# Scores as four 64x64 products per chunk, and sums over channels as two-part products

## The chip, the cores and the metric

The kernel runs on one core of one Trainium2 chip. The metric is the device time of one execution in microseconds (us). Three timed runs of the kernel before gave 2873.15, 2877.79 and 2878.57 us; the median is 2877.79 us. One further execution was recorded by the hardware profiler, and every row below is from that one.

## The reference

One layer of a decoder over 2048 new tokens of one sequence, and over one new token of each of 8 other sequences. In outline:

```
h = rms_norm(x);  P = h @ w_in
branch A (16 heads of 64 channels; state S per head, 64x64, token by token):
  kk = k * k_k;  kk = kk * rsqrt(sum over the head's channels of kk*kk)
  S_t = S_{t-1} diag(w_t) + (S_{t-1} a_t) b_t^T + v_t k_t^T ;  y_t = S_t r_t,   a = -kk, b = kk * iclr
  y = group norm of y over the head's 64 channels
  bonus = (sum over the head's channels of r * k * r_k) * v
  A = ((y + bonus) * silu(z)) @ w_branch_r
branch B: GLU -> depthwise convolution, 31 taps, 512 channels -> layer norm over the 512 channels
  -> swish, * silu(z_c), @ w_branch_c
x + rms_norm((sigmoid(g_r) * A + sigmoid(g_c) * B) @ w_out)
```

So there are five sums over channels: two before the scan of a head and two after it (mean and variance), each over 64 channels, and the layer norm's mean and variance over 512.

## The kernel before

Channels lie on the 128 partitions and tokens along the free axis. The prompt is cut into 4 blocks of 512 tokens. In a block, two heads (128 channels) make a **unit**; there are 8 units in a block and 32 in all, counted here from 0 to 31. For a unit, 8 chunks of 64 tokens each are turned into matrix products.

A unit is one long chain over the engines. Its parts, with the names by which rows show them:

- the low-rank products (`pa<-tw,w`), then sigmoid, scan and exponentials on ScalarE (ACT) and VectorE (DVE);
- the sum of squares of kk (`pa<-tmp,ones_b`), and the sum for the bonus (`pa<-raw,ones_b`), each one product of a 128x128 block of ones with a 128x512 tile: `stat`. The stretch from the end of the unit ahead to this second sum is called the *front* below;
- the scores (`pa<-ar,bk`), masked on DVE into the tiles `sc`; for each chunk and each head one product with 64 rows and 128 columns of weights;
- the inverse of a triangular block: about 45 short instructions on DVE over `gd` and `zr`, at whose end PE continues with `pb<-gd,sc`;
- the *back*: `pb<-zbuf,gp`, `pa<-aw,zbuf`, `pa<-sc,pz`, then the states chunk by chunk (`pc<-xs,aw`), then the mean (`py<-gt,cent`) and the variance (`pc<-gt,ones_b`) of y.

Products on `fp32` tiles go through TensorE (PE) as two instructions. Tiles of type `fp32r` go through as one; exactness is had by splitting a tile into a rounded part and a remainder (`split`: a copy on ACT, a subtraction on DVE). The large projections (`gemm`, rows `pg<-ht,w`) are done so: three products for each pair of 128 rows and columns.

The program is written in the order: unit j, then the projections of unit j+1 (`unit_in`: 4 x 24 products), then what `FILL0`, `FILL1`, `FILL2` list for j: gates (digits, 48 products each), `u` (a GLU), `n` (`conv_norm`, the layer norm), `z` and `Z` (48 products each). A scheduler then orders each engine's instructions by what is ready, and earlier work first; the projections are thereby laid into the times in which the chain of the unit is on ACT and DVE. They are called the **fill** below. PE then runs its list in order.

Buffers are had from pools by tag, in the order of the program: a tag with one buffer (any that `BUFS`, L70, does not list) gives it to the next user when the one ahead has done. PSUM: `pg` has 3 banks (projections and `conv_norm`), `pa` 2, `pb`, `pc` and `py` 1 each.

`conv_norm` (L727) sums four convolution tiles (`cs`) over channels with four products on `avg_c` into one PSUM tile, subtracts the mean, squares each tile on ACT, and sums the squares with four products more. `FILL0` has it behind unit 4 of block 0, the other lists behind unit 2 of their blocks: units 4, 10, 18 and 26.

Of the kernel before, what the change touches and what calls it, by code (L numbers as in the profile page):

```python
# [8 lines left out]
F32 = mybir.dt.float32  # L9
# [16 lines left out]
def rwkv7_conformer_step(  # L26
# [6 lines left out]
    nc = tc.nc  # L33
# [55 lines left out]
    def new(shape, tag, dt=F32):  # L89
        return sb.tile(shape, dt, name=tag, tag=tag, bufs=BUFS.get(tag, 1))  # L90
# [14 lines left out]
    def stt(out, a, s, b, op0, op1):  # L105
        return nc.vector.scalar_tensor_tensor(out=out, in0=a, scalar=s, in1=b, op0=op0, op1=op1)  # L106
# [61 lines left out]
    def cmem(shape, v, name):  # L168
        t = const.tile(shape, F32, name=name)
        nc.gpsimd.memset(t, v)  # L170
        return t
# [5 lines left out]
    ones_b = cmem([128, 128], 0.0, "ones_b")  # L177
    avg_c = cmem([128, 128], 1.0 / DC, "avg_c")
# [36 lines left out]
    cent = const.tile([128, 128], F32, name="cent")  # L215
# [3 lines left out]
    stt(cent, ones_b, -1.0 / 64, ident, ALU.mult, ALU.add)  # L219
# [73 lines left out]
    gate_s = const.tile([128, 2 * KT, NS], F32, name="gate_s")  # L293
    mg_s = const.tile([128, 2, KT, NS], F32R, name="mg_s")
# [79 lines left out]
    def stat(pool, mat, src):  # L374
        ps = pool()
        mm(ps[:, 0:src.shape[1]], mat, src)
        return ps[:, 0:src.shape[1]]

# [92 lines left out]
    def unit(b, j, tw, ins):  # L471
# [4 lines left out]
        w2 = new([128, 3, 128], "w2", F32R)  # L476
        w2r = new([128, 3, 128], "wraw")
        nc.sync.dma_start(out=w2r, in_=w_lora[j])
        cp(w2, w2r)
        tt(w2[:, 2], w2r[:, 2], f32(w2[:, 2]), ALU.subtract)  # L480

        def lora(i):
            ps = pa()
            mm(ps, w2[:, i], tw[:, i], stop=False)
            mm(ps, w2[ES[i], 2], tw[ES[i], i], start=False)
            return ps
# [16 lines left out]
        rsqrt(kkn, stat(pa, ones_b, kkn), eps_kk)  # L503
# [4 lines left out]

        bk = new([128, NC, 3, C], "bk")
        mul(bk[:, :, 0, :], c3(kkn), c3(em))  # L510
        cp(bk[64:128, :, 2, :], bk[64:128, :, 0, :])
# [6 lines left out]
        mul(bonv, stat(pa, ones_b, R), V)  # L518
# [20 lines left out]
        for hf in range(2):  # L539
            pse = [pa(), pa()]  # L540
            for i in range(4):
                c = hf * 4 + i
                for e, es in enumerate(ES):
                    mm(pse[e][:, i * 128:i * 128 + 128], bk[es, c, e:e + 2].rearrange("p a t -> p (a t)"),
                       ar[es, c].rearrange("p a t -> p (a t)"))
            for e in range(2):
                mul(W[hf][:, :, e, :], pse[e].rearrange("p (c t) -> p c t", t=128),
                    maskw.unsqueeze(1).to_broadcast([128, 4, 128]))
# [77 lines left out]
        P = new([128, NC, C], "pz")  # L626
# [49 lines left out]
        pcen = stat(pyt, cent, ys)  # L676
        act(ys, pcen, AF.Square)
        rsqrt(ys, stat(pct, ones_b, ys), eps_gn, scale=1.0 / 64)
# [48 lines left out]
    def conv_norm(b, cs):  # L727
        ps = pgt()
        for ct in range(CT):
            mm(ps, avg_c, cs[ct], start=(ct == 0), stop=(ct == CT - 1))  # L730
        for ct in range(CT):
            tt(cs[ct], cs[ct], ps, ALU.subtract)
        ps = pgt()
        for ct in range(CT):
            sq = new([128, BS], "tmp")
            act(sq, cs[ct], AF.Square)
            mm(ps, avg_c, sq, start=(ct == 0), stop=(ct == CT - 1))
        rs = new([128, BS], "tmp")
        rsqrt(rs, ps, eps_ln)
        for ct in range(CT):  # L740
            mul(cs[ct], cs[ct], rs)
            s1 = new([128, BS], "tmp")
            sigmoid(s1, cs[ct], nscale=nlng[:, ct:ct + 1], nbias=nlnb[:, ct:ct + 1])
            act(cs[ct], cs[ct], AF.Identity, scale=pv("lng", ct), bias=pv("lnb", ct))
            mul(cs[ct], cs[ct], s1)
# [484 lines left out]
```

## Time and profile before

| | |
|---|---|
| median of three runs | 2877.79 us |
| profiled execution | 2879.12 us |
| its span, first to last instruction | 2877.4 us |
| PE busy | 2756.7 us (96%) |
| DVE busy | 1947.1 us (68%) |
| ACT busy | 1343.8 us (47%) |
| mean granted clock of PE | 0.985 |

PE is busy nearly all the time. A PE row `x32` of fp32 products stands for 16 of them, since each is two instructions. In a timeline the starts of rows of one engine tell how long a group took: the duration of a product includes the time until its result has landed, which the next one does not wait for.

### The profile page before, as it was taken

The numbers are of one execution on the slowest core, as the hardware profiler recorded it, in microseconds if no ns is written. First come the engines' busy times: TensorE is split into PE (matmuls) and PEld (weight loads), VectorE is DVE, ScalarE is ACT, GpSimd is POOL, SyncE is SP. The second block draws the span as 40 slices with busy tenths as digits, with TensorE's granted clock in tenths as the row PEclk, the third lists the DMA queues.
The fourth block names the chain that finished last, engine by engine and source line by source line (L and its number), as shares of the span: only waits on it lengthen the run. The fifth ranks groups of instructions, "written<-read, shape, count | busy, mean of one in ns | idle before, by whom it ended". The sixth has DMA issues, their size and how long they took to land.

```text
span 2877.4 us, 53953 instructions
## 1 busy us (share of the span) xinstructions
PE 2756.7 (96%) x21830; PEld 2198.1 (76%) x21830; DVE 1947.1 (68%) x4501; ACT 1343.8 (47%) x2822; POOL 15.6 (1%) x60
## 2 busy tenths in 40 slices
PE   6999899989999999997999999999999999999998
PEld 5888787877877777775787777777798776777777
DVE  5888787767777556676766767665866766566632
ACT  5555556654244455454213446455511446455521
POOL 0000000000000000000000000000000000000000
PEclk9999899999999999997999999999999999999999
DMA  6555554546874324343576334343566532333474
GB/s 236 175 180 186 187 171 133 180 156 210 304 279 131 117 97 159 128 138 107 172 255 208 124 127 138 124 137 100 182 199 218 187 121 77 99 103 118 130 264 160
DMA packets 158285, 468.90 MB, mean 163 GB/s; under 512 B 19857, under 2 KB 25218, under 8 KB 158027
## 3 DMA queue, kind: packets, MB, share of 16 engines
q1 hardware_dynamic: 155665, 456.50, 47.5%
q10 hardware_dynamic: 2370, 8.95, 0.8%
q8 instruction: 172, 2.82, 0.4%
q14 instruction: 78, 0.64, 0.1%
HBM read 352.50 MB, written 113.35 MB: 162 GB/s over the span
## 4 chain that ended last, share of the span: by engine, by line
PE 65%; DVE 20%; ACT 10%; DMA 2%; issue 2%; SPq 0%; POOL 0%; DVEq 0%; ACTq 0%; POOLq 0%
PE pg L112 40%; PE pa L112 12%; PE pc L112 4%; DVE gd L100 4%; DVE zr L576 4%; PE py L112 4%; DVE zr L106 3%; PE pb L112 2%; ACT sc L94 2%; ACT tmp L94 2%; DVE raw L106 1%; ACT zbuf L94 1%; ACT gp L94 1%; ACT gd L94 1%; DVE w L100 1%
## 5 line engine op out<-in xcount | busy, mean ns | idle before, releaser
L112 PE MATMUL pg<-ht,w 128*128 128x512 f32 (+1 forms) x7320 | 1521.4, 361 | 25.2 <-ACT ht L94 7.5
L112 PEld LDWEIGHTS pg<-ht,w 128*128 128x128 f32 x7320 | 1183.2, 189 | 262.3 <-issue 43.9
L106 DVE SCALAR_TENSOR_TENSOR et<-u,cw,et 128x512 f32<-128x512 f32 x480 | 359.3, 748 | 7.5
L94 ACT ACTIVATE raw<-pg,omm 128x512 f32<-128x512 f32 (+1 forms) x160 | 95.9, 600 | 292.9 <-PE pg L112 286.4
L100 DVE TENSOR_TENSOR gd<-zr,gp 128x8 f32<-128x8 f32 (+14 forms) x480 | 179.7, 374 | 12.8
L94 ACT ACTIVATE tmp<-tmp 128x512 f32<-128x512 f32 (+1 forms) x304 | 183.9, 624 | 9.0 <-DVE tmp L492 4.2
L112 PE MATMUL pg<-orr,w 128*128 128x512 f32 (+2 forms) x960 | 186.8, 350 | 0.0
L576 DVE TENSOR_REDUCE zr<-gd 128x2 f32<-128x8 f32 (+14 forms) x480 | 176.6, 368 | 12.3
L94 ACT ACTIVATE w<-wraw 128x512 fp32r<-128x512 f32 (+1 forms) x194 | 117.1, 609 | 129.8 <-PE pg L112 91.8
L112 PEld LDWEIGHTS pg<-orr,w 128*128 128x128 f32 x960 | 154.9, 188 | 25.9 <-issue 0.5
L662 DVE TENSOR_SCALAR xs<-pc,dk 128x64 f32<-128x64 f32 x224 | 63.6, 284 | 142.5 <-PE pc L112 141.8
L112 PEld LDWEIGHTS pa<-ar,bk 64*128 64x128 f32 x1024 | 120.0, 196 | 40.9 <-issue 19.1
L106 DVE SCALAR_TENSOR_TENSOR raw<-pg,prm,raw 128x511 f32<-128x511 f32 (+2 forms) x192 | 106.4, 567 | 52.0 <-ACT raw L94 51.0
L100 DVE TENSOR_TENSOR w<-wraw,w 128x512 fp32r<-128x512 f32 (+1 forms) x194 | 119.6, 621 | 31.3 <-ACT w L94 28.4
L112 PE MATMUL pa<-ar,bk 64*128 64x128 f32 x1024 | 136.1, 294 | 2.5 <-DVE sc L100 2.5
L100 DVE TENSOR_TENSOR aw<-pa,id 128x256 f32<-128x256 f32 x64 | 27.2, 424 | 148.8 <-PE pa L112 148.3
L106 DVE SCALAR_TENSOR_TENSOR zr<-zr,sub 128x5 f32<-128x5 f32 (+7 forms) x512 | 115.7, 226 | 13.4
L94 ACT ACTIVATE gd<-sc 32x128 f32<-32x128 f32 x256 | 78.4, 306 | 83.0 <-DVE sc L100 79.2
L94 ACT ACTIVATE x<-pg 128x512 f32<-128x512 f32 (+1 forms) x80 | 40.8, 511 | 158.8 <-PE pg L112 153.7
L100 DVE TENSOR_TENSOR sc<-pa,maskw 128x512 f32<-128x512 f32 x128 | 87.0, 688 | 34.3 <-PE pa L112 33.2
L94 ACT ACTIVATE sc<-pa 64x256 f32<-64x256 f32 (+1 forms) x192 | 72.9, 380 | 52.6 <-PE pb L112 49.6
L100 DVE TENSOR_TENSOR x<-x,pg 128x512 f32<-128x512 f32 (+1 forms) x80 | 46.1, 578 | 71.9 <-PE pg L112 59.5
(331 smaller groups left out, 3686.4 us busy)
## 6 DMA issues: line engine op xcount, KB each, us to landing
w<-kept_in SPq DMA_DIRECT2D x366, 512.0 KB, 3.3
kept_in<-w SPq DMA_DIRECT2D x122, 512.0 KB, 4.5
wraw<-in_w_in_dram SPq DMA_DIRECT2D x122, 256.0 KB, 3.1
w<-kept_br SPq DMA_DIRECT2D x48, 512.0 KB, 3.6
w<-kept_out SPq DMA_DIRECT2D x40, 512.0 KB, 4.4
gate<-x SPq DMA_DIRECT2D x64, 256.0 KB, 3.3
x<-gate SPq DMA_DIRECT2D x64, 256.0 KB, 4.2
orr<-in_x_prompt_dram SPq DMA_DIRECT2D x24, 512.0 KB, 6.7
```

Source lines behind the costliest of these rows:

```text
L94: return nc.scalar.activation(out=out, in_=in_, func=func, scale=scale, bias=bias, **kw)
L100: return nc.vector.tensor_tensor(out=out, in0=a, in1=b, op=op)
L106: return nc.vector.scalar_tensor_tensor(out=out, in0=a, scalar=s, in1=b, op0=op0, op1=op1)
L112: return nc.tensor.matmul(out=out, lhsT=lhsT, rhs=rhs, start=start, stop=stop, **kw)
L576: nc.vector.tensor_reduce(out=zr[:, 0:n, t:t + 2], in_=pr[:, 0:n, :, 0:w], axis=AX.X, op=ALU.add)
L662: nc.vector.tensor_scalar(out=state[:, j, :] if c == NC - 1 else xs[:, c + 1, :], in0=pu[:, c * C:c * C + C], scalar1=dk[:, c:c + 1], scal ...
```

## The change

Four parts:

1. `stat2` takes the place of `stat` for the four sums of a unit: the source is split into two `fp32r` parts in a tile `st` (one buffer), and two products take the place of one on fp32.
2. The scores: for each chunk and head two products of 64x64 weights instead of one of 64x128. The copy on ACT that put one operand in a second place goes.
3. `conv_norm` adds its four tiles (and then their four squares) on DVE, and makes one `stat2` of each sum.
4. The low-rank weights lie in a constant tile whose unused quarters are zero; `P` of a unit takes the tag `gt` in place of one of its own.

```diff
@@ lora weights and two-part constants @@
-    cent = const.tile([128, 128], F32, name="cent")
+    cent_r = const.tile([128, 128], F32R, name="cent")
...
+    lora_w = const.tile([128, 4, 128], F32R, name="lora_w")
+    nc.gpsimd.memset(f32(lora_w), 0.0)
...
+    def stat2(pool, mat, src):
+
+        parts = new([128, 2, BS], "st", F32R)
+        split(parts[:, 0], parts[:, 1], src)
+        ps = pool()
+        for i in range(2):
+            mm(ps, mat, parts[:, i], start=(i == 0), stop=(i == 1))
+        return ps
@@ unit @@
-        w2 = new([128, 3, 128], "w2", F32R)
+        w2 = lora_w
         w2r = new([128, 3, 128], "wraw")
         nc.sync.dma_start(out=w2r, in_=w_lora[j])
-        cp(w2, w2r)
-        tt(w2[:, 2], w2r[:, 2], f32(w2[:, 2]), ALU.subtract)
+        cp(w2[:, 0:2], w2r[:, 0:2])
+        for i, es in enumerate(ES):
+            tt(w2[es, 2 + i], w2r[es, 2], f32(w2[es, i]), ALU.subtract)
...
-            mm(ps, w2[ES[i], 2], tw[ES[i], i], start=False)
+            mm(ps, w2[:, 2 + i], tw[:, i], start=False)
...
-        rsqrt(kkn, stat(pa, ones_b, kkn), eps_kk)
+        rsqrt(kkn, stat2(pa, ones_r, kkn), eps_kk)
...
-        bk = new([128, NC, 3, C], "bk")
+        bk = new([128, NC, 2, C], "bk")
         mul(bk[:, :, 0, :], c3(kkn), c3(em))
-        cp(bk[64:128, :, 2, :], bk[64:128, :, 0, :])
...
-        mul(bonv, stat(pa, ones_b, R), V)
+        mul(bonv, stat2(pa, ones_r, R), V)
...
-                for e, es in enumerate(ES):
-                    mm(pse[e][:, i * 128:i * 128 + 128], bk[es, c, e:e + 2].rearrange("p a t -> p (a t)"),
-                       ar[es, c].rearrange("p a t -> p (a t)"))
+                for q in range(2):
+                    for e, es in enumerate(ES):
+                        mm(pse[e][ES[e ^ q], i * 128:i * 128 + 128], bk[es, c, q, :],
+                           ar[es, c].rearrange("p a t -> p (a t)"))
...
-        P = new([128, NC, C], "pz")
+        P = new([128, NC, C], "gt")
...
-        pcen = stat(pyt, cent, ys)
+        pcen = stat2(pyt, cent_r, ys)
         act(ys, pcen, AF.Square)
-        rsqrt(ys, stat(pct, ones_b, ys), eps_gn, scale=1.0 / 64)
+        rsqrt(ys, stat2(pct, ones_r, ys), eps_gn, scale=1.0 / 64)
@@ conv_norm @@
-        ps = pgt()
-        for ct in range(CT):
-            mm(ps, avg_c, cs[ct], start=(ct == 0), stop=(ct == CT - 1))
+        sm = new([128, BS], "tmp")
+        tt(sm, cs[0], cs[1], ALU.add)
+        for ct in range(2, CT):
+            tt(sm, sm, cs[ct], ALU.add)
+        ps = stat2(pgt, avg_r, sm)
         for ct in range(CT):
             tt(cs[ct], cs[ct], ps, ALU.subtract)
-        ps = pgt()
-        for ct in range(CT):
+        sm = new([128, BS], "tmp")
+        act(sm, cs[0], AF.Square)
+        for ct in range(1, CT):
             sq = new([128, BS], "tmp")
             act(sq, cs[ct], AF.Square)
-            mm(ps, avg_c, sq, start=(ct == 0), stop=(ct == CT - 1))
+            tt(sm, sm, sq, ALU.add)
+        ps = stat2(pgt, avg_r, sm)

```

How this moves PE's instructions in block 3, from the sum for the bonus of unit 26 to the end of its inverse. Before:

```order
L112 MATMUL pa<-raw,ones_b 128x512
L112 MATMUL pa<-ar,bk 128x128 x8
L112 MATMUL pg<-ht,w 128x512 x2
L112 MATMUL pa<-ar,bk 128x128 x8
L112 MATMUL pg<-ht,w 128x512 x6
L112 MATMUL pa<-ident,ar 64x64 x16
L112 MATMUL pa<-xv,sc 64x64 x16
L617 MATMUL pa<-ident,bk 128x128 x4
L112 MATMUL pg<-ht,w 128x512 x2
L617 MATMUL pa<-ident,bk 128x128 x4
L112 MATMUL pg<-ht,w 128x512 x85
L112 MATMUL pb<-gd,sc 32x32 x16
```

After, on PE, from the mean of unit 25 to the same place and two rows past it:

```order
L112 MATMUL py<-st,cent 128x512 x2
L112 MATMUL pc<-st,ones_b 128x512 x2
L112 MATMUL pa<-st,ones_b 128x512 x4
L112 MATMUL pa<-ar,bk 64x128 x32
L112 MATMUL pa<-ident,ar 64x64 x16
L112 MATMUL pa<-xv,sc 64x64 x16
L630 MATMUL pa<-ident,bk 128x128 x8
L112 MATMUL pb<-gd,sc 32x32 x16
L112 MATMUL pb<-zbuf_183,gp 32x32 x16
L112 MATMUL pa<-aw,zbuf_183 64x128 x16
```

The rows `pg<-ht,w`, the fill, stood at four places of this stretch, 95 products in all; there is none now.

The second place is `conv_norm` of block 3 on PE. Before, its first four products stood by the end of the inverse of unit 25:

```order
L112 MATMUL pg<-ht,w 128x512 x66
L112 MATMUL pg<-et,avg_c 128x512
L112 MATMUL pb<-gd,sc 32x32 x16
L112 MATMUL pg<-et,avg_c 128x512 x2
L112 MATMUL pb<-zbuf_184,gp 32x32 x16
L112 MATMUL pg<-et,avg_c 128x512
L112 MATMUL pa<-aw,zbuf_184 64x128 x16
```

After, it stands behind the variance of unit 26, a whole unit later, and the fill follows it:

```order
L112 MATMUL pc<-xs,aw 64x64 x2
L112 MATMUL py<-aw,xs 64x64 x2
L112 MATMUL py<-st,cent 128x512 x2
L112 MATMUL pc<-st,ones_b 128x512 x2
L112 MATMUL pg<-st,avg_c 128x512 x4
L112 MATMUL pg<-ht,w 128x512 x82
```

The DVE rows of the same place, after, with the tiles' numbers: `st` is the tile of `stat2`, and the three users of it here are the mean of unit 26, its variance, and the first sum of `conv_norm` (`tmp_25063`, whose additions stand a unit earlier on DVE).

```order
L675 TENSOR_SCALAR state_189<-pc_24768,dk_24465 128x64
L100 TENSOR_TENSOR st_24844<-gt_24842,st_24844 128x512
L100 TENSOR_TENSOR st_24851<-gt_24842,st_24851 128x512
L100 TENSOR_TENSOR st_25067<-tmp_25063,st_25067 128x512
L100 TENSOR_TENSOR gt_24842<-py_24847,gt_24842 128x512
L100 TENSOR_TENSOR et_21745<-et_21745,pg_25070 128x512
```

The split of that sum has moved behind the two sums of the unit, because the one buffer of `st` goes round in the order of the program.

The third place is the scores on PE, after, with numbers (the second half of unit 27's scores and a part of the first; `pa_25196` and `pa_25216` are one head, `pa_25197` and `pa_25217` the other):

```order
L112 MATMUL pa_25196<-ar_25161,bk_25164 64x128 x3
L112 MATMUL pa_25175<-st_25172,ones_b_92 128x512
L112 MATMUL pa_25196<-ar_25161,bk_25164 64x128 x5
L112 MATMUL pg_25678<-ht_21600,w_25676 128x512 x2
L112 MATMUL pa_25197<-ar_25161,bk_25164 64x128 x8
L112 MATMUL pa_25216<-ar_25161,bk_25164 64x128 x7
L112 MATMUL pa_25217<-ar_25161,bk_25164 64x128 x7
L112 MATMUL pa_25216<-ar_25161,bk_25164 64x128
L112 MATMUL pa_25217<-ar_25161,bk_25164 64x128
```

The products of one head stand one behind another, up to eight in a row; heads alternate only in the last two.

## Rows read from the trace of the kernel before

**Rows 1.** The page, part 1: busy us, share of the span, instructions.

```profile
PE 2756.7 (96%) x21830; PEld 2198.1 (76%) x21830; DVE 1947.1 (68%) x4501; ACT 1343.8 (47%) x2822; POOL 15.6 (1%) x60
```

**Rows 2.** Waits of PE: what waited for what, total us, times, longest.

```profile
PE pb L112 <- DVE gd L580: 13.7, 18, 3.4
```

**Rows 3.** Windows: start:end, us, busy us per engine, PEclk, DMA share, GB/s.

```profile
0.00:120.00 120.00, 90.24 (x783) 85.31 (x785) 77.59 (x209) 64.17 (x141) 5.50 (x30) 1.00 0.66 229
2621.10:2677.90 56.80, 55.43 (x505) 42.08 (x507) 34.20 (x86) 31.62 (x65) 0.34 (x1) 1.00 0.37 119
1308.20:1346.60 38.40, 25.35 (x279) 17.17 (x279) 18.32 (x36) 24.48 (x52) 0.34 (x1) 0.72 0.12 44
```

**Rows 4.** Timeline of PE, unit 30 and the inverse of unit 31.

```profile
2621.09 0.69 PE L112 MATMUL pb<-gd,sc 32*32 32x32 f32 x32 [0.43 <-DVE gd L580]
...
2643.46 9.38 PE L112 MATMUL pg<-ht,w 128*128 128x512 f32 x38
2652.94 1.12 PE L112 MATMUL pa<-raw,ones_b 128*128 128x512 f32 x2
...
2661.61 15.34 PE L112 MATMUL pg<-ht,w 128*128 128x512 f32 x65
2677.86 0.69 PE L112 MATMUL pb<-gd,sc 32*32 32x32 f32 x32 [0.91 <-DVE gd L580]
```

**Rows 5.** Windows, only instructions that name the tile ht.

```profile
2621.10:2677.90 56.80, 32.42 (x127) 23.36 (x127) 0.00 (x0) 0.00 (x0) 1.00 0.37 119
1308.20:1346.60 38.40, 3.30 (x6) 1.66 (x6) 2.58 (x4) 2.38 (x4) 0.72 0.12 44
```

**Rows 6.** Timeline of PE, end of unit 14 and front of unit 15.

```profile
1308.19 1.06 PE L112 MATMUL pb<-gd,sc 32*32 32x32 f32 x32 [3.44 <-DVE gd L580]
...
1332.24 1.02 PE L112 MATMUL pa<-tmp,ones_b 128*128 128x512 f32 x2
...
1344.72 1.91 PE L112 MATMUL pa<-raw,ones_b 128*128 128x512 f32 x2
1346.56 3.09 PE L112 MATMUL pa<-ar,bk 64*128 64x128 f32 x16
```

**Rows 7.** The chain that ended last, by time: start, us, what.

```profile
1133.88 0.86 PE py L112 x2
1134.74 1.17 PE pg L112 x5
...
1137.62 10.67 PE pg L112 x46
```

**Rows 8.** Groups of PE by form: busy us, mean ns, idle before.

```profile
L112 PE MATMUL pa<-raw,ones_b 128*128 128x512 f32 x64 | 36.8, 659 | 7.2 <-DVE raw L106 6.5
...
L112 PE MATMUL pg<-tmp,avg_c 128*128 128x512 f32 x32 | 20.2, 736 | 8.5 <-ACT tmp L94 8.5
...
L112 PE MATMUL pg<-et,avg_c 128*128 128x512 f32 x32 | 15.6, 606 | 0.0
```

**Rows 9.** Timeline of PE, scores of one unit and what follows.

```profile
1086.76 4.01 PE L112 MATMUL pa<-ar,bk 64*128 64x128 f32 x32
1090.70 1.03 PE L112 MATMUL pa<-ident,ar 64*64 64x64 f32 x28
```

**Rows 10.** Timeline of PE, 64x64 products with 128 columns moving.

```profile
1058.95 2.15 PE L112 MATMUL pa<-sc,pz 64*64 64x128 f32 x32
1061.03 1.15 PE L112 MATMUL pc<-xv,sc 128*64 128x64 f32 x30
```

**Rows 11.** Timeline of PE, two sorts of 64x64 products side by side.

```profile
2659.45 0.22 PE L112 MATMUL pa<-xv,sc 64*64 64x64 f32 x1
2659.46 0.22 PE L112 MATMUL pa<-ident,ar 64*64 64x64 f32 x1
```

**Rows 12.** Groups by form, ACT and DVE: a 128x512 split.

```profile
L100 DVE TENSOR_TENSOR w<-wraw,w 128x512 fp32r<-128x512 f32 x162 | 110.7, 687 | 29.5 <-ACT w L94 26.7 <-PE pa L112 1.6 <-PE pb L112 0.3
L94 ACT ACTIVATE w<-wraw 128x512 fp32r<-128x512 f32 x162 | 101.1, 627 | 129.3 <-PE pg L112 91.8 <-DMA wraw<-in_w_in_dram 16.6 <-DMA kept_out<-w 9.4
```

More of the change, by code (lines that the diff above doesn't have):

```diff
@@ L166, in rwkv7_conformer_step, with cmem @@
     make_identity(nc, ident)
-    def cmem(shape, v, name):
-        t = const.tile(shape, F32, name=name)
-        nc.gpsimd.memset(t, v)
+    def cmem(shape, v, name, dt=F32):
+        t = const.tile(shape, dt, name=name)
+        nc.gpsimd.memset(f32(t) if dt == F32R else t, v)
         return t
@@ L176, in rwkv7_conformer_step @@
     eps_kk = cmem([128, 1], 1e-12, "eps_kk")
-    ones_b = cmem([128, 128], 0.0, "ones_b")
-    avg_c = cmem([128, 128], 1.0 / DC, "avg_c")
+    ones_b = f32(ones_r := cmem([128, 128], 0.0, "ones_b", F32R))
+    avg_c = f32(avg_r := cmem([128, 128], 1.0 / DC, "avg_c", F32R))
     rms_d = [dram.tile([4, 128], F32, name=f"rms{b}") for b in range(NB)]
@@ L218, in rwkv7_conformer_step @@
         nc.gpsimd.memset(ones_b[s, s], 1.0)
-    stt(cent, ones_b, -1.0 / 64, ident, ALU.mult, ALU.add)
+    stt(cent_r, ones_b, -1.0 / 64, ident, ALU.mult, ALU.add)
+    cent = f32(cent_r)
     id2 = const.tile([128, C], F32, name="id2")
```

## The prediction

> **What bounds the kernel now.** I read the page's engine line first: PE is busy 2756.7 of 2877.4 us [rows 1], so 120.7 us are idle. Of these 29.8 lie in the first 120 us [rows 3], the start. The waits of PE come next: the longest kind in the units is for the end of the triangular inverse on DVE, 18 times, 13.7 us together [rows 2]. So PE is full, yet it waits a little for the chain of nearly every unit: the chain is as long as the work laid beside it. The timeline of one unit shows that. From the end of one inverse to the end of the next 56.8 us pass [rows 4], with PE busy for 55.43 [rows 3]: 1.4 idle, 45 us in 32 units. In that time 127 projections run as fill [rows 5]: 38 in the front, 65 beside the inverse [rows 4], some 3 by the scores, the other 21 in the back. At 10.67/46 = 0.232 us each [rows 7] the fill is 29.5 us, the unit's own products 26. Without fill the chain would still need its 56.8 us, and PE would idle for some 29.5.
>
> The trace has one place that is nearly so, the end of block 1 [rows 6]: 38.4 us with 6 projections [rows 5], PE busy 25.35 and so 13 us idle, at a granted clock of 0.72 [rows 3], that is part of it at 1.2 GHz and not 2.4. That is the picture to keep: where fill is missing PE waits, and its clock falls too.
>
> **PE's work.** A sum over channels takes 0.86 us on fp32 [rows 7]; two fp32r products take 0.47 at the 1.17/5 = 0.234 us of the projections in the same rows. That is 0.39 us, for 4 sums x 32 units = 128 (64 instructions a group are 32 sums, and there are four such groups, [rows 8]): **-50 us**. `conv_norm` has 8 fp32 products in each of 4 blocks (64 instructions in the two groups, [rows 8]); 32 x 0.86 = 27.5 becomes 16 x 0.234 = 3.7: **-24 us**.
>
> Scores: now 32 instructions from 1086.76 to 1090.70, 0.123 us each [rows 9]; then 64. The nearest form shown is a 64x64 product with 128 columns moving, two quadrants in turn: 2.08/32 = 0.065 us [rows 10], so 4.2 us a unit for 3.9, +7 us in all. If all four quadrants ran at once, half of 0.065 would hold: 2.1 us, -58 us in all. That quadrants of two sorts can be in flight together the trace shows: products on the diagonal quadrants and on the other two start 0.01 us apart [rows 11]. But the order puts the eight products of one head behind one another, and they use one half of the rows. I take 0, between the two and near the row with the same form.
> The Trainium skill, TensorEngine Tiling (Array Packing), section Tiling Modes, says that four 64x64 tiles are independent and load and multiply in parallel. By that rule the scores would come to the -58 us; rows 11 agree as far as they go, and it is a rival below.
>
> The low-rank products stay two a sum (128 rows and not 64, the same columns), the split's subtraction is two instructions for one, and a copy on ACT of half a tile goes: 0 us, beside PE's work in the filled units; if that cover is gone a few tenths of a us a unit.
>
> **The chain.** Each `stat2` puts a copy on ACT (0.63 us) and a subtraction on DVE (0.69 us) [rows 12] before its product: 1.3 us of chain, four times in a unit, 5.2 us. In a unit with enough fill PE does not see it: it takes some 23 more projections in the same time. But the fill is a fixed amount, so it is used up sooner. A unit without any fill now idles 29.5 + 5.2 = 35 us: by parts back 4.9 + 2.6 = 7.5, front 38 x 0.232 + 2.6 = 11.5, scores 1, inverse 65 x 0.232 = 15.
>
> **Where fill is missing.** This is the step on which the forecast rests, and the order shows it. `st` has one buffer, handed on in program order, so `conv_norm` can split its first sum only when the unit ahead of it in the program has done its variance, at the very end of its back. The projections that come later in the program stand behind `conv_norm` in the order, so nothing is left to fill with in that unit. Before, `conv_norm` took its first products straight from the convolution's tiles, an inverse and a back earlier. Its own chain, bare, adds about 7 us of idle PE: two splits, four subtractions of 0.69, a square and an addition, less its products. Counting the fill in the new order, place by place, against the needs above:
> - block 0: unit 4's back empty, then `conv_norm`: 7.5 + 7 = 14.5.
> - block 1: unit 10's front has 20 projections (4.7 of 11.5), scores and inverse none, back none, `conv_norm`: 6.8 + 1 + 15 + 7.5 + 7 = 37.
> - block 2: the same at unit 18, front 25 (5.8): 5.7 + 1 + 15 + 7.5 + 7 = 36.
> - block 3: unit 25's front 13 (3.0) and back none, unit 26 none at all, `conv_norm`: 8.5 + 7.5 + 11.5 + 1 + 15 + 7.5 + 7 = 58.
> - ends of blocks, where less is left: some 5 us each at the back of unit 6, the front of 7, the inverse of 14 and the back of 31; 7.5 at each of the backs of 14 and 22; 2.7 and 10.8 at the fronts of 15 and 23: 48.
>
> Sum 194 us. The kernel before idles 120.7 - 29.8 - 45 = 46 us outside start and ordinary units, of which I put 35 at these places (13 are those of [rows 6]). So **+159 us** idle. The clock: in [rows 6] 16 score instructions took 3.09 us, where 32 take 3.94 [rows 9]: 1.1 us for half the scores. With a few such losses at each of four to seven places, an estimate from those rows, **+12 us**.
>
> Bounds of this term: nothing below 0, if the empty stretches cost no more than those of before; above, 194 with no credit for the old ones and twice the clock, some 220.
>
> DVE gains 128 subtractions and 4 x 8 additions and splits, some 110 us on 1947; ACT 128 copies less 32: neither becomes a bound.
>
> **Sum.** 2879.1 (the profiled execution) - 50 - 24 + 0 + 159 + 12 = 2976; that execution lies 1.3 us above the median, so **2975 us**, 3.4% slower.
>
> **Rivals.**
> - *The work cut is got in full.* PE is 96% busy and most units are full, which speaks for it: 2879 - 74 = 2805. For that the empty units must be as short as their own products, some 25 us, and not 60. Against it: the inverse alone is 15 us of bare DVE time, and rows 6 show PE idle where the fill was thin. This is the case on the other side of no change, and it decides from the point where the extra idle is under 74 us. 0.14.
> - *Four quadrants at once*, -58 us: 2917. For it rows 11, against it the order by heads and the mask on DVE that must free a `pa` bank. 0.12.
> - *The empty stretches cost half.* The bare chain, with no projection's evacuation between its DVE and ACT instructions, may run much faster than in filled units: 2879 - 74 + 80 + 6 = 2891, and with the spread of that, 2860 to 2920. 0.12: half slower, the rest shared by the same and faster.
> - The forecast itself, 2930 to 3030: 0.62.
>
> Within 0.2% of the median is what a measurement of this kernel can't tell from no change. Faster: 0.14 + 0.03 = 0.17; same 0.03; slower 0.62 + 0.12 + 0.06 = 0.80. The range of 2850 to 3040 leaves out the first rival and a part of the upper bound.
>
> **What would show it.** Right: PE's busy time falls by some 70 us or more, yet its share falls to about 90%, with idle stretches of 15 us and more before `pb<-gd,sc` in units 10, 18 and 26, and before `pa<-st` in their fronts; the granted clock well under 0.985. Each sum takes 0.47 us, the scores 3.5 to 4.2 us a unit. The distance from inverse to inverse in full units rises from 57 to some 62 us. Wrong: no gap over 10 us before `pb<-gd,sc` there, or scores near 2 us a unit.

## Result: slower by 6.1%, and the profile after

The changed kernel takes 3054.36 us (median of 4 runs, 3050.37 to 3056.63) where the kernel before took 2878.18 in the same comparison: 1.0613 times as long, 95% interval 1.0594 to 1.0631. The prediction was 2975 us with a range of 2850 to 3040, and the time lies 14 us above it. The side was right, the size too small: 176 us were lost where 97 were forecast.

The profiled execution took 3054.28 us, its span is 3052.6 us and the mean granted clock 0.938 (0.985 before). The engine line of the page and its row of the clock in 40 slices:

```profile
PE 2746.8 (90%) x22806; PEld 2223.3 (73%) x22806; DVE 2066.9 (68%) x4693; ACT 1396.9 (46%) x2926; POOL 16.1 (1%) x61
PEclk9999988979999879998999978998899986999989
```

Against [rows 1], PE is busy 9.9 us less and idle 3052.6 - 2746.8 = 305.8 us where it was 120.7, so 185.1 more; less the 9.9 that is the difference of the spans, 175.2. But "busy" hides the clock. In the trace the stretches granted at 1.2 GHz sum to 380 us (90 before), some 2 us of them behind the last instruction (the means agree: (1 - 0.938)/0.5 x 3052.6 = 379), and PE is busy in 215 us of them (70 before). Half of that busy time is taken here as what the lower clock adds, 107 us against 35. It is an estimate: projections in a row start 0.427 us apart at 1.2 GHz and 0.232 at 2.4, a little less than twice. So the account is: work at full clock -82, lower clock +72, idle +185. Where "full-clock work" and "lower clock" are named for other runs below, they are worked out in the same way.

PE's waits, in the columns of [rows 2]:

```profile
PE pb L112 <- DVE gd L593: 83.6, 19, 15.0
PE pa L112 <- ACT st L94: 36.5, 19, 7.8
PE pg L112 <- ACT st L94: 34.8, 8, 7.4
PE pa L112 <- ACT zbuf L94: 17.4, 29, 1.3
...
PE pc L112 <- ACT st L94: 14.3, 10, 2.0
PE py L112 <- ACT st L94: 14.2, 8, 1.8
```

The wait for the inverse on DVE went from 13.7 to 83.6 us, with a longest of 15.0 where it was 3.4. Of the other rows shown all but one name `st`, the tile of the two parts, which did not exist before; they come to 99.8 us. With the 69.9 us at the inverse that is 170 of the 185 us. The timeline of PE shows both at one place of block 3, the inverse and the end of unit 26 and the `conv_norm` behind it:

```profile
2546.65 1.77 PE L630 MATMUL pa<-ident,bk 128*128 128x128 f32 x8
2563.09 1.06 PE L112 MATMUL pb<-gd,sc 32*32 32x32 f32 x32 [14.67 <-DVE gd L593]
...
2584.11 0.49 PE L112 MATMUL py<-st,cent 128*128 128x512 f32 x1 [1.82 <-ACT st L94]
...
2586.68 1.52 PE L112 MATMUL pc<-st,ones_b 128*128 128x512 f32 x2 [1.35 <-ACT st L94]
2589.50 1.52 PE L112 MATMUL pg<-st,avg_c 128*128 128x512 f32 x2 [1.29 <-ACT st L94]
2598.44 1.52 PE L112 MATMUL pg<-st,avg_c 128*128 128x512 f32 x2 [7.42 <-ACT st L94]
2599.76 0.63 PE L112 MATMUL pg<-ht,w 128*128 128x512 f32 x1
```

`conv_norm`'s first product (`pg<-st,avg_c`) comes right behind the variance of the unit ahead (`pc<-st,ones_b`), its second 9 us later, and only then the next projection. Nothing fills the 14.67 us beside the inverse. The same wait at unit 18, another answer of that view, and its return to normal one inverse later:

```profile
1813.26 1.06 PE L112 MATMUL pb<-gd,sc 32*32 32x32 f32 x32 [15.03 <-DVE gd L593]
1912.12 0.69 PE L112 MATMUL pb<-gd,sc 32*32 32x32 f32 x32 [0.57 <-DVE gd L593]
```

Now windows: the first row, for comparison, is a full unit, the others lie in the stretches around unit 26 (columns as in [rows 3]):

```profile
2851.30:2914.20 62.90, 61.56 (x567) 47.63 (x567) 38.26 (x91) 35.57 (x71) 0.34 (x1) 1.00 0.47 162
2520.00:2540.00 20.00, 7.97 (x40) 4.20 (x39) 14.56 (x24) 10.90 (x21) 0.00 (x0) 0.52 0.00 0
2540.00:2563.00 23.00, 7.59 (x104) 6.77 (x104) 18.45 (x54) 3.65 (x10) 0.00 (x0) 0.57 0.00 1
2583.00:2603.00 20.00, 8.60 (x17) 4.85 (x18) 11.33 (x18) 9.91 (x18) 0.00 (x0) 0.57 0.00 0
```

In the three empty stretches PE is busy for 33 to 43% of the time, at a clock of 0.52 to 0.57: most of each is at 1.2 GHz. How much of the idle time lies at the four `conv_norm` is shown by four longer windows, from the inverses of units 3, 9, 17 and 24 to those of units 5, 11, 19 and 27:

```profile
363.50:539.80 176.30, 142.00 (x1486) 126.50 (x1485) 128.55 (x319) 98.64 (x201) 0.68 (x2) 0.87 0.40 134
1015.30:1178.80 163.50, 124.91 (x1119) 97.23 (x1118) 97.25 (x232) 84.73 (x175) 0.34 (x1) 0.84 0.32 93
1748.40:1912.10 163.70, 125.53 (x1097) 96.79 (x1097) 106.94 (x245) 84.95 (x175) 0.67 (x2) 0.82 0.31 100
2435.60:2657.70 222.10, 163.93 (x1553) 125.03 (x1553) 134.81 (x315) 107.47 (x221) 1.01 (x3) 0.82 0.21 70
```

PE idles 34.3, 38.6, 38.2 and 58.2 us in them, 169 us together; before, the same four stretches held 23 us.

The full unit has its clock and 1.3 us of idle time, but it is longer. In the kernel before the two last periods from inverse to inverse were 56.8 us [rows 4] and, from 2677.86 there, 58.3:

```profile
2736.18 0.69 PE L112 MATMUL pb<-gd,sc 32*32 32x32 f32 x32 [0.91 <-DVE gd L580]
```

After, they are 63.2 and 62.9 us. Of the same view, with what answers to [rows 7, 9]:

```profile
2788.20 0.69 PE L112 MATMUL pb<-gd,sc 32*32 32x32 f32 x32 [0.68 <-DVE gd L593]
...
2851.37 0.69 PE L112 MATMUL pb<-gd,sc 32*32 32x32 f32 x32 [1.06 <-DVE gd L593]
...
2871.07 0.39 PE L112 MATMUL py<-st,cent 128*128 128x512 f32 x1
2871.30 0.62 PE L112 MATMUL pg<-ht,w 128*128 128x512 f32 x2
...
2891.14 1.59 PE L112 MATMUL pa<-ar,bk 64*64 64x128 f32 x32
2892.67 0.73 PE L112 MATMUL pg<-ht,w 128*128 128x512 f32 x2
...
2914.28 0.69 PE L112 MATMUL pb<-gd,sc 32*32 32x32 f32 x32 [0.91 <-DVE gd L593]
```

One part of a sum takes 0.23 us, two of them 0.47. Thirty-two score instructions take 1.53 us, 0.048 each; with the smaller groups between projections, the 64 of the unit come to some 3.7 us. One by one, their starts in the trace come in pairs, 0.007 us apart, and a pair follows the one before after 0.109 us. The pairs follow after 0.045 to 0.064 us in one stretch only, where the second 16 instructions have begun and the first 16 are not yet through. The products of [rows 10] also start in pairs 0.007 us apart, 0.109 us from pair to pair.

One group was not looked at in the prediction, the low-rank products. Of the kernel before, by form, busy us and mean ns:

```profile
L112 PE MATMUL pa<-tw,w 64*128 64x512 f32 x64 | 31.8, 496 | 0.0
L112 PE MATMUL pa<-tw,w 128*128 128x512 f32 x64 | 31.5, 493 | 0.0
```

And of the kernel after:

```profile
L112 PE MATMUL pa<-tw,lora_w 128*128 128x512 f32 x128 | 52.0, 461 | 0.0
```

The sum fell from 63.3 to 52.0 us when the second product of each pair read all 128 rows, half of its weights being zero.

### The profile page after: what moved, and what is told of

The parts are those of the page before. It is cut to its first block, busy times and chain, and to the rows that moved or that the text cites. A ratio compares the mean times of both kernels' runs of the same rounds, so it can differ in the third digit from the quotient of the medians.

```text
span 3052.6 us, 56274 instructions
## 1 busy us (share of the span) xinstructions
PE 2746.8 (90%) x22806; PEld 2223.3 (73%) x22806; DVE 2066.9 (68%) x4693; ACT 1396.9 (46%) x2926; POOL 16.1 (1%) x61
## 4 chain that ended last, share of the span: by engine, by line
PE 60%; DVE 22%; ACT 13%; issue 2%; DMA 2%; SPq 0%; another core or an unknown queue 0%; POOL 0%; DVEq 0%; ACTq 0%; POOLq 0%
PE pg L112 38%; PE pa L112 12%; DVE gd L100 5%; DVE zr L589 4%; PE pc L112 4%; PE py L112 4%; DVE zr L106 3%; PE pb L112 2%; ACT tmp L94 2%; ACT sc L94 2%; DVE raw L106 1%; DVE et L106 1%; ACT gt L94 1%; ACT zbuf L94 1%; ACT xv L94 1%
## 5 line engine op out<-in xcount | busy, mean ns | idle before, releaser
L112 PE MATMUL pg<-ht,w 128*128 128x512 f32 (+1 forms) x7320 | 1505.8, 358 | 21.4 <-DVE sconv L109 5.2
L112 PEld LDWEIGHTS pg<-ht,w 128*128 128x128 f32 x7320 | 1196.8, 191 | 228.7 <-issue 13.0
L100 DVE TENSOR_TENSOR gd<-zr,gp 128x8 f32<-128x8 f32 (+14 forms) x480 | 179.6, 374 | 12.6
L589 DVE TENSOR_REDUCE zr<-gd 128x2 f32<-128x8 f32 (+14 forms) x480 | 176.5, 368 | 12.6
L94 ACT ACTIVATE w<-wraw 128x512 fp32r<-128x512 f32 x162 | 101.3, 628 | 135.4 <-PE pg L112 104.7
L112 PE MATMUL pa<-ar,bk 64*64 64x128 f32 x2048 | 143.4, 302 | 4.8 <-DVE sc L100 4.7
L112 PEld LDWEIGHTS pa<-ar,bk 64*64 64x64 f32 x2048 | 111.7, 146 | 40.4 <-issue 20.4
L100 DVE TENSOR_TENSOR w<-wraw,w 128x512 fp32r<-128x512 f32 x162 | 110.6, 686 | 28.6 <-ACT w L94 27.3
L106 DVE SCALAR_TENSOR_TENSOR zr<-zr,sub 128x5 f32<-128x5 f32 (+7 forms) x512 | 115.6, 226 | 13.7
L112 PE MATMUL pa<-aw,zbuf 64*64 64x128 f32 x1024 | 87.6, 307 | 18.0 <-ACT zbuf L94 17.4
```

Of the source, the lines that this page charges most:

```text
L94: return nc.scalar.activation(out=out, in_=in_, func=func, scale=scale, bias=bias, **kw)
L100: return nc.vector.tensor_tensor(out=out, in0=a, in1=b, op=op)
L112: return nc.tensor.matmul(out=out, lhsT=lhsT, rhs=rhs, start=start, stop=stop, **kw)
L589: nc.vector.tensor_reduce(out=zr[:, 0:n, t:t + 2], in_=pr[:, 0:n, :, 0:w], axis=AX.X, op=ALU.add)
```

## Experiments

Theory A: the one buffer of `st`, handed on in program order, holds `conv_norm` back and empties the units beside it. Theory B: the two further steps ahead of each unit sum lengthen the chain of every unit. The others are named where they come up. Times are medians, each beside runs of the kernel before on the same chip (2875.9 to 2877.0 us).

**`conv_norm`'s parts in `tmp`.** The changed kernel, with

```diff
-        ps = stat2(pgt, avg_r, sm)
+        hi, lo = new([128, BS], "tmp", F32R), new([128, BS], "tmp", F32R)
+        split(hi, lo, sm)        # then two products, as in stat2
```

> The changed kernel, with one difference: conv_norm's two parts lie in two tiles of the tag tmp and no longer in st, so that its split needn't wait for the variance of the unit ahead. Theory A (the queue for the one st buffer empties the four units beside a conv_norm): the four periods that grew by 24 to 34 us lose most of that, the half clock in them goes with it, and the time falls by 100 to 140 us to 2915 to 2955 us. Theory B (the longer chain of each unit, four splits of about 1.3 us on ACT and DVE, is what costs): the four units give back little, and the time stays above 3010 us. Theory C (conv_norm's additions on DVE are the delay, whatever the buffer): the units beside a conv_norm stay as they are, 3040 us or more.

Measured 2969.04 us, 85 less than the changed kernel; half clock 277 us. PE's first products behind the inverses of units 25, 26 and 27:

```profile
2439.50 0.69 PE L112 MATMUL pb<-gd,sc 32*32 32x32 f32 x32 [2.53 <-DVE gd L593]
...
2510.31 0.69 PE L112 MATMUL pb<-gd,sc 32*32 32x32 f32 x32
2574.96 0.69 PE L112 MATMUL pb<-gd,sc 32*32 32x32 f32 x32 [0.64 <-DVE gd L593]
```

From unit 26's inverse to the next 64.7 us pass. The same distance in the changed kernel, from 2563.09 to the row

```profile
2657.67 0.69 PE L112 MATMUL pb<-gd,sc 32*32 32x32 f32 x32 [0.39 <-DVE gd L593]
```

was 94.6. So A is real, and worth some 85 us, under its forecast of 100 to 140; theory C falls as the main cause, and 92 us above the kernel before stay to be explained. In the four stretches around a `conv_norm` PE's idle time falls from 169 to 60 us, but 39 us of idle time come up elsewhere: the fill that these units take up again is missing in others.

**`conv_norm` as before.** The changed kernel with the old function, 64 fp32 instructions in all.

> The changed kernel with conv_norm's products as they were before (32 of 0.86 us a block in place of four of 0.23 us), so st is used by the unit sums alone. Theory A: the units beside a conv_norm get their products back, as in the run with the tag tmp, less the 24 us of work that the change had taken out: 2935 to 2980 us. Theory B: above 3010 us. Theory C: as A, since the additions are gone too; it then lies well below the run with the tag tmp.

2970.10 us: the same as with `tmp`. The queue is gone either way, and the rest of the loss is elsewhere.

**Unit sums as before.** Four `stat2(...)` back to `stat(...)`.

> The changed kernel with the four sums of each unit as plain fp32 products again; st then holds conv_norm's parts alone, and the scores stay as four 64x64 products. Theory A alone: st is free whenever conv_norm wants it, so the same 100 to 140 us come back, plus nothing for the units: 2915 to 2955 us, and the full units stay at about 63 us. Theory B alone: the units' chains are short again (about 57 us for a full unit), and the conv places stay as they are: 2920 to 2960 us. A and B both: both amounts come back, 2840 to 2880 us, with the clock near 0.985.

2862.34 us, 0.9955 [0.994, 0.997] of before: both amounts come back. So the two-part sums of the units, directly and through `st`, account for the whole loss. PE's wait for the inverse is normal again:

```profile
PE pg L112 <- ACT st L94: 23.4, 4, 9.5
...
PE pb L112 <- DVE gd L593: 12.0, 17, 2.0
```

**Scores alone.** The kernel before, without the copy on ACT that the new form needs no more, and with

```diff
-                    mm(pse[e][:, i * 128:i * 128 + 128], bk[es, c, e:e + 2]..., ar[es, c]...)
+                for q in range(2):
+                    for e, es in enumerate(ES):
+                        mm(pse[e][ES[e ^ q], i * 128:i * 128 + 128], bk[es, c, q, :], ar[es, c]...)
```

> The kernel before with the scores as four 64x64 products of 128 columns in place of two of 64x128 into 128x128, and without the copy of the third plane of bk; nothing else. The prediction's nought: 2870 to 2886 us, scores of a unit 3.5 to 4.2 us from the first to the last. Rival with four quadrants side by side: each unit gains 1.8 us of its chain, about 2820 us. Rival where the 2048 products (143 ns busy each in the changed kernel, against 136 ns for half as many before) keep PE longer: up to 2890 us.

2864.06 us, 0.9959 [0.9947, 0.997]: a gain of 13 us, not 58, and not nothing. (The 143 and 136 of the last rival are the busy us of all these instructions together, not ns of one.) PE's work at full clock is the same (2722 and 2725 us); idle time fell by 5 us and the time at half clock from 90 to 62 us. Whether that comes from the order of the products or from ACT's copy that went too was not tried.

**Wait without saving.** The run with `tmp`, where each unit sum is one fp32 product behind two further steps:

```diff
-        split(parts[:, 0], parts[:, 1], src)   # and two fp32r products
+        cp(parts[:, 0], src)
+        tt(parts[:, 1], src, parts[:, 0], ALU.max)
+        return stat(pool, f32(mat), parts[:, 1])
```

> The run with conv_norm's parts in tmp, with each of the four unit sums again one fp32 product of 0.86 us, but of a tile that first goes through ACT (a copy) and DVE (the larger of copy and source), as the two parts did: the delay of the split stays, the work that it saved on TensorE does not. Theory B (the delay in the chain is what costs, 107 us between the runs with and without the unit sums' splits): 2965 to 3020 us, full units 62 to 65 us. Theory D (the units are slow because TensorE has less to do beside the chain and loses its clock): TensorE's work is back, so the time goes to 2860 to 2890 us.

3009.16 us. Theory D falls: with PE's full-clock work up by 33 us again (50 were forecast for the sums) the kernel is slower still, by 40 us, and not faster.

**Load without wait.** As the last, but with `return stat(pool, f32(mat), src)`.

> The run with the delayed fp32 sums, with one difference: the four sums of a unit read the source itself and no longer wait for the copy on ACT and the comparison on DVE, which are still made, into a tile that nothing reads. The load on ACT and DVE stays, the wait of the sums goes. Theory B (it is the sums' waiting for two further steps that costs): most of the way back to the kernel without splits, 2865 to 2895 us. Theory E (the eight further instructions of a unit on ACT and DVE, 5.3 us, are in the way wherever they stand): 2985 to 3010 us, as with the wait.

2899.13 us, 110 us less, by the waits alone; it is 4 us above B's range. Of the 117 us between the two profiled executions 79 are idle time and 40 lower clock, with PE's work 2 us the other way. The products behind the inverses of units 29 and 30, with the wait:

```profile
2739.79 0.69 PE L112 MATMUL pb<-gd,sc 32*32 32x32 f32 x32 [0.98 <-DVE gd L591]
2805.51 0.69 PE L112 MATMUL pb<-gd,sc 32*32 32x32 f32 x32 [0.93 <-DVE gd L591]
```

and without:

```profile
2643.93 0.69 PE L112 MATMUL pb<-gd,sc 32*32 32x32 f32 x32 [0.66 <-DVE gd L591]
2703.24 0.69 PE L112 MATMUL pb<-gd,sc 32*32 32x32 f32 x32 [0.89 <-DVE gd L591]
```

65.7 us and 59.3: 6.4 us in this stretch, and 4.2 on average over the five from unit 26 on (65.5 and 61.4), near the 5.2 us of four copies and subtractions [rows 12]. PE idles about 1 us at either place. This shows directly that the sums' waits cost, and that full PE does not mean that PE sets the pace.

It does not show that each sum waits for its own two further steps, as theory B has it. In the same five stretches, on average and against the run without the wait, the mean of y comes 1.8 us later behind the last state product, the variance 0.9 us later behind the mean, the sum of kk 2.3 us later behind the variance, and the bonus sum 1.0 us sooner behind that of kk. The sum of kk needs nothing of the variance. Its rows in the run with the wait:

```profile
2760.40 0.71 ACT L94 ACTIVATE tmp<-raw,prm 128x512 f32<-128x512 f32 x1
...
2764.08 1.13 PE L112 MATMUL pc<-st,ones_b 128*128 128x512 f32 x2 [0.15 <-DVE st L100]
...
2765.83 0.62 ACT L94 ACTIVATE st<-tmp 128x512 f32<-128x512 f32 x1
...
2767.23 1.13 PE L112 MATMUL pa<-st,ones_b 128*128 128x512 f32 x2
```

Its source (`tmp<-raw,prm`) is ready at 2761.1, but its copy into `st` starts 4.7 us later, when the variance's product has read the one buffer. So a part of the cost in every unit, some 2 of the 4.2 us, is again the queue for `st`, as in theory A. That is read from these rows; no run with a second buffer tried it.

**No split at all.** Each unit sum one fp32r product, with the low part of its operand left out.

> The run with conv_norm's parts in tmp, with each of the four unit sums one fp32r product of 0.23 us whose operand the producing instruction writes in that type; the low part of the operand is left out of the sums. No split stands in the chain, and 0.63 us a sum of TensorE's work are gone against fp32 (128 times, 81 us). Theory B: full units fall to 54 to 56 us and the time to 2770 to 2810 us. Theory D (less work beside the chain costs the clock, and gives the gain back): full units stay at 57 us or more, half clock rises above 150 us, 2830 to 2870 us.

2820.86 us. It lies between the two ranges, 78 us below the run without splits further on (2898.45 us, of which the low-rank products are a part): most of the 81 us of work counts, but full units end at 57.9 us

```profile
2624.89 0.69 PE L112 MATMUL pb<-gd,sc 32*32 32x32 f32 x32 [0.92 <-DVE gd L591]
...
2682.82 0.69 PE L112 MATMUL pb<-gd,sc 32*32 32x32 f32 x32 [0.90 <-DVE gd L591]
```

and not at 54 to 56, and half clock is 147 us. Four products shorter by 0.63 us each shorten a full unit by some 1.2 us, not 2.5 (the last four periods are 58.5 us on average, and 59.7 in the run without splits). What holds it there was not tried.

**One of four, three of four.** The run with `tmp`, only the bonus sum in two parts, or only the other three.

> The run with conv_norm's parts in tmp, with three of the four unit sums (of the squares of kkn, cent and the variance) as fp32 products again; only the bonus sum, whose result the unit needs at its end alone, is in two parts. Theory B (only a split in the chain costs): the bonus split is hidden, and 32 times 0.39 us of work go: 2845 to 2862 us. Rival, that each split costs its share of the 107 us wherever it stands: 2880 to 2895 us.

> The run with conv_norm's parts in tmp, with the bonus sum as an fp32 product and the other three unit sums in two parts. Theory B: these three carry the whole cost, 2960 to 2985 us. Rival, equal shares: about 2942 us.

2882.38 and 2940.02 us: on the face of it equal shares, and B's "the bonus is free" wrong. But the kernel with none in two parts and `conv_norm` in `tmp` takes 2898.45 us:

**Scores and `conv_norm` in `tmp`.** No unit sum in two parts.

> The kernel before with the four 64x64 score products and with conv_norm's tiles added on DVE, its two parts in tmp; unit sums in fp32. Against the kernel with the scores alone (2864 us): theory A (additions on DVE cost nothing when no queue for st is there) 2840 to 2866 us, 24 us of TensorE's work being gone. Theory C (the additions and the split leave TensorE empty at conv_norm): 2870 to 2890 us, and then the bonus sum's own cost, in the run with 2882 us, is the smaller for it.

2898.45 us, 34 above the scores alone, more than C expected. Against it the bonus sum in two parts is 16 us faster, the other three are 42 slower, and all four 71 slower; some 6 to 17 us of each difference are the low-rank products, which this run has as before (see below). The shares do not add up, and what the bonus costs the whole kernel is open. In full units it costs next to nothing: the last four periods are 59.7 us on average with no sum in two parts, 59.9 with the bonus alone, 62.3 with the other three and 63.0 with all four. Of this kernel's 34 us, 20 lie behind the start of the last inverse (158.6 us to the end; 138.4 with the scores alone, 133 to 148 in the other runs), with one wait that I did not trace further:

```profile
PE pg L112 <- DVE x L100: 10.6, 1, 10.6
```

**Added work in the holes.** The changed kernel, with

```diff
+        if u in (4, 10, 18, 26):
+            dp = pct()
+            for _ in range(90):
+                mm(dp, cent_r, lora_w.rearrange("p a b -> p (a b)"))
```

> The changed kernel with 90 products of 128x512 (0.22 us each, results never read) added in each of the units 4, 10, 18 and 26, in the stretches that a conv_norm leaves empty: 79 us of further work on TensorE. Theory F (the lower clock in and behind the empty stretches is a cost of its own, 72 us of the 176): half clock falls from 380 us to 300 us or less and the time falls, by 15 to 40 us to 3015 to 3040 us, although work is added. If the clock there costs nothing, since the chain in those stretches waits for ACT and DVE: 3050 us or more.

3030.68 us, 1.0545 [1.0524, 1.0567] of before: 24 us faster than the changed kernel with more work on PE (its full-clock work rises by 93 us). Half clock falls to 256 us. PE's timeline in front of unit 26's inverse:

```profile
2512.34 8.33 PE L112 MATMUL pc<-lora_w,cent 128*128 128x512 f32 x36
...
2526.50 10.51 PE L112 MATMUL pc<-lora_w,cent 128*128 128x512 f32 x45
2546.80 1.06 PE L112 MATMUL pb<-gd,sc 32*32 32x32 f32 x32 [6.61 <-DVE gd L598]
```

Half of the busy time at the lower clock falls from 107 to 79 us, and idle time by 81. So the lower clock costs time of its own (theory F). It is not the only thing that changed: in block 0, 69 projections moved from before unit 4's inverse to behind it. In block 2 the same products stand before unit 18's inverse as without them, in nearly the same order, and that inverse comes 3.0 us sooner (61.9 us for 64.9 from the one ahead). The clock is not all to be had back: the distance from unit 25's inverse to this one stays at 63.5 us (2483.28 to 2546.80, before 2499.51 to 2563.09), since there DVE's inverse comes last.

**A version that beats both.** Unit sums single, `conv_norm`'s means in fp32 as before, and

```diff
-            sq = new([128, BS], "tmp")
+            sq = new([128, BS], "tmp", F32R)
-            mm(ps, avg_c, sq, start=(ct == 0), stop=(ct == CT - 1))
+            mm(ps, avg_r, sq, start=(ct == 0), stop=(ct == CT - 1))
```

> A version meant to beat both: four 64x64 score products, the unit sums as single fp32r products (low parts left out), conv_norm's means as fp32 products as before, its squares as single fp32r products of tiles that ACT writes in that type; no split and no addition on DVE anywhere. Against the run with single products and the additions on DVE (2821 us): theory C (the additions leave TensorE empty at conv_norm, 23 us of waits for ACT's tmp there) 2795 to 2815 us; if conv_norm's chain costs nothing there, 2821 us plus the 14 us of work that its products take more, 2830 to 2840 us.

2808.36 us, 0.9766 [0.9742, 0.979] of before, with the low parts left out. It does 11 us more of full-clock work than the single sums with DVE's additions and is 12 us faster. Its wait at `conv_norm`:

```profile
PE pg L112 <- ACT tmp L94: 14.3, 8, 5.7
```

and that of the other:

```profile
PE pg L112 <- ACT tmp L94: 23.2, 8, 7.8
```

Then four runs to price the parts one by one.

**Low-rank products alone.** `lora_w` with zeros, on the kernel before.

> The kernel before with the low-rank products alone changed: the second of each sum over all 128 rows, with zeros for the other half, in place of 64 rows. TensorE's busy time in these products was 63.3 us before and 51.7 us in kernels with the change. The prediction's nought: 2872 to 2882 us. Rival, that the shorter product counts, since TensorE is full: about 12 us less, 2862 to 2869 us.

2866.49 us, 0.9969 [0.9957, 0.998]: the 11 us count, though nothing in the chain was shortened by more than some tenths of a us a unit.

**Scores and low-rank products.**

> The kernel before with the four 64x64 score products (2864 us alone) and the low-rank products over 128 rows; unit sums and conv_norm as before. If the low-rank products count: 2848 to 2857 us, the fastest without a sum that leaves anything out. If not: 2861 to 2868 us.

2858.48 us, 0.9946 [0.993, 0.9963]: the fastest that leaves nothing out. Of the 11 us some 6 come on top of the scores'; the interval is too wide to say more.

**The four splits, nothing else in `st`.**

> Scores and the four unit sums in two parts in st, conv_norm and the low-rank products as before: the four splits with nobody else in the queue for st. Theory B (the splits' waits): 2970 us with the low-rank products changed, so 2970 to 2985 us here, 106 to 120 us above the kernel with the scores alone. If the low-rank products' zeros had been a part of the loss (the two further subtractions of a unit on DVE): under 2965 us.

2987.17 us, 123 above the scores alone: the four splits cost 123 us net, though they take 49 us of full-clock work off PE; idle time rises by 101 and the lower clock by 69. The zeros of the low-rank products are no part of the loss: the same kernel with them is the run with `conv_norm` as before, and 17 us faster. This run and the next have `P` in `gt`, as the changed kernel has and the scores alone have not; what that tag is worth was not tried by itself.

**`conv_norm` in `st`, alone there.**

> Scores and conv_norm with its additions on DVE and its parts in st, which nothing else uses; unit sums in fp32 and the low-rank products as before. With them changed it was 2862 us. If those count: 2870 to 2877 us, so that conv_norm's edit costs some 10 us against the scores alone (2864 us). If not: 2859 to 2866 us, and conv_norm's edit is worth nothing either way, for 24 us forecast.

2879.25 us, 15 above the scores alone and 17 above the run with the low-rank products changed (2862 us): `conv_norm`'s edit costs time even where no unit sum stands in the queue ahead of its parts, and the low-rank products are worth 17 us here.

## Why the prediction was right in direction and wrong in size

Step by step, the forecast's terms against what was measured:

- **PE's work, -50 and -24.** As work it was right: -82 at full clock, of which 11 are the low-rank products that the prediction put at nothing. A sum in two parts takes 0.47 us, as forecast. As time, neither was got: the unit sums' edit costs 123 us alone, `conv_norm`'s 15. Both savings were bought with further steps on ACT and DVE ahead of PE's products. The low-rank products' 11 us, bought with one more subtraction a unit, on weights only, came in full.
- **Scores, 0.** 3.7 us a unit, inside the 3.5 to 4.2 named. The products are faster one by one than [rows 10] let expect (0.048 us for 0.065), far from the half that four quadrants at once would give over the whole unit. The rule of the Trainium skill, TensorEngine Tiling (Array Packing), section Tiling Modes, was a rival with -58 us; the run with the scores alone gave -13. What the trace shows of its parallel work is two instructions at a time (pairs 0.109 us apart) for most of the scores, and about twice that pace (0.045 to 0.064 us) in the short stretch where two groups meet. That fits the prediction's reason against the rival, the order by heads.
- **The chain, 5.2 us a unit.** Right in size: full units grew by 6.4 and 4.6 us, and the pair of runs with and without the wait shows 4.2 us on average. That it came out so near is in part luck. It was put together from four splits of 1.3 us; in that pair the bonus' split adds nothing, the mean's and the variance's 1.8 and 0.9 us, and the sum of kk 2.3 us, by its place in the queue for `st` and not by its length.
- **Where fill is missing, +159.** The places and the cause were right. The holes of some 15 us stand before the inverses of units 10, 18 and 26 (14.90, 15.03 and 14.67), as named; in the fronts the longest wait for `st` is 7.8 us and not 15. Blocks 1, 2 and 3 idle 38.6, 38.2 and 58.2 us around their `conv_norm`, for 37, 36 and 58 forecast. Block 0 idles 34.3 for 14.5, with a hole of 12.5 us before unit 4's inverse that was not named, and the five stretches at the ends of blocks 67 for 48. Putting `conv_norm`'s parts elsewhere brings 85 us back. PE's additional idle time is 185 us, 26 above the sum and inside its bound of 220.
- **The clock, +12.** This is the step that failed, a term of the sum that was mis-sized: it measured +72, and with it go 60 of the 78 us by which the change of the span exceeds the forecast of 97; the idle time gives 26 more, and 8 more of work went off. The prediction took the loss from one row, 16 score instructions of [rows 6], and multiplied it by four to seven places; the upper bound doubled it to 24 us only. The window beside it had the right number: 38.4 us at 0.72 are 38.4 x 0.28/0.5 = 21.5 us at half clock [rows 3], and with PE busy 25.35 of 38.4 that is, by this estimate, 21.5 x 0.66/2 = 7.1 us lost for 13 us idle, 0.55 us for each (in the trace PE is busy in 12.6 us of that half clock, 0.48 for each). The change cost 72 for 185, or 0.39; at such rates 159 us of idle time carry 60 to 90 us of clock with them. The added products show that it is a cost and not only a sign: the kernel became 24 us faster with them.

The rivals: the work cut was not got at all, since each of the two savings came with steps of ACT and DVE ahead of PE's products. The gain of four quadrants at once did not come: the pace that it would need shows only in a short stretch of the scores above. That the empty stretches cost half did not happen either; they cost more than the forecast. What a size for theory A and for theory B is apart can be given only by differences: 85 us for the queue (the changed kernel against `tmp`), 106 to 123 for the splits (with the low-rank products' gain and without). A chain of four runs, each with one part more, leads from one kernel to the other: the scores -13 (2864.06), the unit sums with `P` in `gt` +123 (2987.17), the low-rank products -17 (2970.10), `conv_norm` +84 (3054.36). In another order the shares are others: `conv_norm` costs 15 us without the units' splits, and the low-rank products are worth 6 to 17. A second buffer for `st`, which might take both queues away, was not tried.

## What to carry to other kernels

- An engine that is 96% busy need not be what sets the pace: ask whether the work laid beside the chain would simply be laid elsewhere. If so, steps added to the chain lengthen every full round (4.2 us here), and the kernel pays where the work so used up is missing (79 us of idle time and 40 of lower clock for these waits). Work taken off the engine at the price of such steps gave nothing here (49 us off, 123 us lost); work taken off without them did count (11 us for 11).
- Idle time of PE is to be priced with the clock that goes with it, from a window's granted clock and busy time and not from single instructions: here 0.4 to 0.55 us for each. It is not a fixed price: against the kernel before, the single sums have 60 us more idle time and 8 us more lower clock, the four splits alone 96 and 58.
- Before a new tile tag with one buffer is used by two parts of a program, look at which of them the ring's order puts last, and at two users within one part too: the sum of kk waited for the variance of the unit ahead.

## What was not expected of the hardware

- More work made the kernel faster: with 360 products whose results nobody reads it took 24 us less. The estimated loss at the lower clock fell from 107 to 79 us; a moved part of the fill in block 0 has a share in it that was not separated.
- A pair of low-rank products over 128 and 64 rows costs more than a pair over 128 rows with half of the second's weights zero: 63.3 us of busy time against 52.0 in 64 pairs, 0.18 us a pair, and 11 us of the kernel's time. The Trainium skill, TensorEngine Tiling (Array Packing), section Tiling Modes, says that a change of the tiling mode drains TensorE; the rows fit that, since the pair went from 128 to 64 rows before and no longer does, but no run here separates that from other reasons.
- The instructions of 64x64 products with 128 columns start in pairs, 0.007 us apart and 0.109 us from pair to pair, in the scores as in [rows 10]; where two groups of scores meet, the pairs follow after 0.045 to 0.064 us, as if all four quadrants ran at once. Over a row of 32 that makes 0.048 us each, against 0.065 in [rows 10], whose row holds a longer gap. An order that alternates the heads throughout was not tried.
